# A gate matrix product by seven block products, with block sums on GpSimd, in a two-layer decoder trunk

## The chip, the cores and the metric

The kernel runs on one core of a Trainium2 chip. A core has five engines that run their own instruction queues side by side: PE (matrix products), DVE (VectorE), ACT (ScalarE), POOL (GpSimd) and SP (SyncE, which here issues the transfers). They share an on-chip memory, SBUF; PE writes to another, PSUM, in banks of 128 x 512 floats that DVE and ACT read. The metric is the time of one execution on the device in microseconds.

## The reference

The reference runs 512 tokens of width 1024 through two layers. Each layer mixes tokens (layer 0 with a state-space mixer, layer 1 with HGRN2), norms, runs a two-matrix MLP of width 4096 with a squared ReLU, norms again, and adds a gated embedding:

```
h = layer_norm(ALPHA * x + mix, ...)
h = layer_norm(ALPHA * h + sq_relu_mlp(h, w1, w2), ...)
x = h + sigmoid(h @ ple_w_gate) * (p @ ple_w_proj)
```

The change is to the last line: the gate h @ ple_w_gate is 512x1024 by 1024x1024, the embedding p @ ple_w_proj is 512x256 by 256x1024. All is float32.

## The kernel before

**A product in three matmuls.** A float32 operand is split into a high part (a cast to a reduced float32 format) and a low part (the operand less its high part). A product is three matmuls, high by high, high by low and low by high (`mm3`, L115 to L118), all accumulated in one PSUM bank. A weight arrives as 128x1024 pieces ("units"): SP loads one into a `raw` buffer, of which there are three; ACT casts it to `whi` (L110); DVE subtracts to `wlo` (L112). There are six `whi` and six `wlo` buffers.

**The MLP's second product** already goes by blocks. Two rows by two columns of blocks take seven block products in place of eight (Strassen's method in Winograd's form): sums of blocks of the weights (`weight_sums`, t1 to t4, made in place in `r` buffers) and of the activations (`half_blocks`: a11, a12, a22 and the sums s1 to s4) are multiplied, and banks accumulate several products each. All its sums are made on DVE. In the last of four rounds the layer norm of token chunks 0 and 1 (128 tokens each) starts while the last of these block products still run on PE (`after(0), after(1)`), and that of chunks 2 and 3 follows.

**The layer norm** of a chunk is a mean and a sum of squares, then two DVE operations over 128x1024 (L220, L221). Then PE transposes the chunk in eight transposes to the banks `pt` and `pm`, ACT casts each bank to the high part (L235) and DVE subtracts to the low part (L236). Chunk 0 is transposed within the last block product (`turns`), chunk 1 within the embedding products, chunks 2 and 3 within the gate's first products (`turned`).

**The gate, before.** For each half h of the 1024 columns, and each of four chunks c, 8 x 3 matmuls of 512 columns make the gate in a bank `pj`. ACT takes the sigmoid (L485), DVE multiplies with the embedding's bank (L486, where `pp` is `py` or `pj`) and adds to the accumulator `acc` (L489). The embedding product `proj` takes 2 x 3 matmuls. In layer 0 the result is turned for the next mixer (L443 to L447) one piece late; in layer 1 it goes out to memory. The very last piece in layer 1 is done in two parts of 256 columns.

**What sets the order.** Each engine runs its instructions in a fixed order, set when the kernel is built. `tc.high_priority(offset=n)` moves the instructions inside it ahead of those that were written up to n earlier: `LEAD` (100) for units, `SUMS` for weight sums, `TURN` (200) for the transposes' splits, `SOON` (40) for the norm. A buffer or bank that is reused waits until its last reader is done. POOL does nothing but fill a few constants.

Of the kernel before, what the change touches and what calls it, by code (L numbers as in the profile page):

```python
# [29 lines left out]
TURN = 200  # L30

# [10 lines left out]
def trunk(ctx: ExitStack, tc, a):  # L42
# [63 lines left out]
    def split(f, lead=LEAD):  # L106
        n = f.shape[1]
        with tc.high_priority(offset=lead):
            hi = mk(whip, [P, 1024], "whi", F32R)
            nc.scalar.copy(hi[:, :n], f)  # L110
            lo = mk(wlop, [P, 1024], "wlo", F32R)
            nc.vector.tensor_sub(lo[:, :n], f, f32(hi[:, :n]))  # L112
        return hi, lo
# [171 lines left out]

# [25 lines left out]
    def weight_sums(w, lead):  # L311
# [7 lines left out]
        with tc.high_priority(offset=lead):  # L319
            for u in range(2):  # L320
                load(0, u, w[0][1][u])
                load(2, u, w[1][1][u])
                nc.vector.tensor_sub(t[2][u], t[2][u], t[0][u])
                load(1, u, w[0][0][u])
                nc.vector.tensor_sub(t[0][u], t[0][u], t[1][u])
                nc.vector.tensor_add(t[1][u], t[2][u], t[1][u])
            for u in range(2):
                load(3, u, w[1][0][u])
                nc.vector.tensor_sub(t[3][u], t[3][u], t[1][u])
# [52 lines left out]
    def mlp_and_gate(layer, h_s, last):  # L382
# [66 lines left out]
        pps = {}  # L449

        def proj(c, pu):

            pp = pps[c] = bank(*((psj, "pj") if c > 1 and pps else (psy, "py%d" % (c % 2))))
            for k in range(2):
                ks = slice(k * 512, (k + 1) * 512)
                mm3(pp, p_s[0][:, k, c * P : (c + 1) * P], p_s[1][:, k, c * P : (c + 1) * P], pu[0][:, ks], pu[1][:, ks], k == 0, k == 1)

        for h in range(2):
            pu = unit(a[f"wp_{layer}"][h])
            gu = [unit(a[f"wg_{layer}"][4 * h + j]) for j in range(4)]  # L460
            for c in range(NCH):
                sl = slice(c * P, (c + 1) * P)
                if h == c == 0:
                    for i in range(NCH):
                        proj(i, pu)
                        if i == 1:
                            turned(1)
                if h == 1:
                    proj(c, pu)
                pp = pps.pop(c)  # L470
                pg = bank(psj, "pj")
                sg = tmp("sg", [P, T])
                parts = 2 if last and h == 1 and c == NCH - 1 else 1
                for i in range(parts):
                    n = 512 // parts
                    if i:
                        pg = bank(psj, "pj")
                    cs = slice(i * n, (i + 1) * n)
                    for k in range(8):
                        ks = slice((k % 2) * 512 + i * n, (k % 2) * 512 + (i + 1) * n)  # L480
                        mh, ml = gu[k // 2][0][:, ks], gu[k // 2][1][:, ks]
                        mm3(pg[:, cs], h_s.h(k, sl), h_s.l(k, sl), mh, ml, k == 0, k == 7)
                        if h == 0 and c < 2 and k == 2:
                            turned(c + 2)
                    nc.scalar.activation(sg[:, cs], pg[:, cs], AF.Sigmoid)  # L485
                    nc.vector.tensor_mul(sg[:, cs], pp[:, cs], sg[:, cs])  # L486
                    fs = slice(h * 512 + i * n, h * 512 + (i + 1) * n)
                    d = acc[:, c, fs]
                    nc.vector.tensor_add(d, sg[:, cs], d)  # L489
                    if last:  # L490
                        nc.sync.dma_start(a["out"][c * P : (c + 1) * P, fs], d)
                while late:
# [790 lines left out]
```

## Time and profile before

| | us |
|---|---|
| median of three runs (1422.39 to 1423.45) | 1422.39 |
| profiled execution | 1422.3 |
| its span | 1420.5 |
| PE busy | 1413.6 |
| DVE busy | 1025.4 |
| ACT busy | 744.4 |
| POOL busy | 1.6 |
| gate stage, layer 0 | 704.0 to 764.5 |
| gate stage, layer 1 | 1358 to the end |

The span runs from the first to the last instruction on the profile; the profiled execution's own time is 1.8 us longer. "Busy" is the time in which an engine had an instruction running. Several matmuls overlap, so their rate is read from the distance of their starts and not from the duration of one. A row of the profile names a line of the kernel, an engine, an operation, the output and inputs with their shapes, how many, their time and what ended the wait before them.

### The profile page before, as it was taken

Reading aid. Unit: us, or ns where it says so; the run is one execution under the profiler, and the core shown is the slowest. Engines: PE = TensorE matmul, PEld = TensorE weight load, DVE = VectorE, ACT = ScalarE, POOL = GpSimd, SP = SyncE. Lnnn points to the kernel's source line nnn. Section 1 sums busy time; section 2 is a strip of 40 time slices with the busy share of each in tenths; the row PEclk is TensorE's granted clock in tenths of the full one; section 3 lists DMA queues with packets and bytes.
Section 4 is the critical chain, followed back from the end, with each engine's and each line's share of the span. In section 5 each row is a group of like instructions: output and inputs, shape, how many; then the busy total and the mean of one; then the engine's idle time right before and its main releaser. Section 6 shows DMA issues by size and latency. Waiting matters only on the chain.

```text
span 1420.5 us, 20454 instructions
## 1 busy us (share of the span) xinstructions
PE 1413.6 (100%) x8143; PEld 1182.3 (83%) x8143; DVE 1025.4 (72%) x1713; ACT 744.4 (52%) x1089; POOL 1.6 (0%) x9
## 2 busy tenths in 40 slices
PE   9999999999999999999999999999999999999998
PEld 7888888888888888888888888888898888888887
DVE  7987777778967667677963774776785867667873
ACT  7776656664265454545543446465454544544641
POOL 0000000000000000000000000000000000000000
PEclk9999999999999999999999999999999999999999
DMA  8343333233433444442422222222163444444231
GB/s 292 127 145 108 113 118 101 95 104 124 158 119 127 156 133 149 134 148 104 149 90 91 92 92 72 90 90 76 60 238 104 148 147 135 149 133 163 89 119 45
DMA packets 48960, 174.83 MB, mean 123 GB/s; under 512 B 5728, under 2 KB 6368, under 8 KB 48736
## 3 DMA queue, kind: packets, MB, share of 16 engines
q1 hardware_dynamic: 48864, 173.52, 35.9%
q8 instruction: 64, 1.05, 0.3%
q14 instruction: 32, 0.26, 0.1%
HBM read 171.34 MB, written 2.16 MB: 122 GB/s over the span
## 4 chain that ended last, share of the span: by engine, by line
PE 96%; DVE 2%; DMA 1%; ACT 0%; issue 0%; SPq 0%
PE pj L116 25%; PE pj L118 25%; PE pj L117 25%; PE py L116 5%; PE py L118 5%; PE py L117 5%; PE py L687 1%; PE py L942 1%; PE pm L669 1%; PE py L689 1%; PE pt L635 0%; PE pt L230 0%; DMA acc<-in_xw 0%; PE pm L230 0%; DVE wlo L112 0%; DVE b L236 0%
## 5 line engine op out<-in xcount | busy, mean ns | idle before, releaser
L110 ACT CAST whi<-raw 128x1024 fp32r<-128x1024 f32 x226 | 237.1, 1050 | 377.8 <-PE pj L117 264.6
L112 DVE TENSOR_TENSOR wlo<-raw,whi 128x1024 fp32r<-128x1024 f32 x226 | 274.3, 1220 | 159.1 <-ACT whi L110 155.0
L116 PE MATMUL pj<-b,whi 128*128 128x512 f32 (+1 forms) x1008 | 381.5, 379 | 0.2 <-ACT b L235 0.2
L117 PE MATMUL pj<-b,whi 128*128 128x512 f32 (+1 forms) x1008 | 379.4, 376 | 0.7 <-DVE b L236 0.7
L118 PE MATMUL pj<-b,wlo 128*128 128x512 f32 (+1 forms) x1008 | 378.9, 376 | 0.0
L118 PE MATMUL pj<-whi,b 128*128 128x512 f32 (+1 forms) x592 | 229.5, 388 | 0.0
L116 PE MATMUL pj<-whi,b 128*128 128x512 f32 (+1 forms) x584 | 229.3, 393 | 0.0
L117 PE MATMUL pj<-wlo,b 128*128 128x512 f32 (+1 forms) x584 | 226.1, 387 | 0.0
L116 PEld LDWEIGHTS pj<-b,whi 128*128 128x128 f32 x1008 | 189.5, 188 | 36.2 <-issue 1.7
L118 PEld LDWEIGHTS pj<-b,wlo 128*128 128x128 f32 x1008 | 189.8, 188 | 34.7
L117 PEld LDWEIGHTS pj<-b,whi 128*128 128x128 f32 x1008 | 189.8, 188 | 34.6 <-DVE b L236 0.9
L118 PEld LDWEIGHTS pj<-whi,b 128*128 128x128 f32 x592 | 111.3, 188 | 22.9 <-DVE b L1137 0.2
L116 PEld LDWEIGHTS pj<-whi,b 128*128 128x128 f32 x584 | 109.8, 188 | 22.7 <-ACT k L871 0.5
L117 PEld LDWEIGHTS pj<-wlo,b 128*128 128x128 f32 x584 | 109.8, 188 | 21.2
L110 ACT CAST whi<-r 128x1024 fp32r<-128x1024 f32 x64 | 67.4, 1053 | 63.8 <-PE pj L118 35.6
L112 DVE TENSOR_TENSOR wlo<-r,whi 128x1024 fp32r<-128x1024 f32 x64 | 78.0, 1219 | 22.2 <-ACT whi L110 22.0
L118 PE MATMUL py<-whi,b 128*128 128x512 f32 x216 | 84.2, 390 | 0.0
L117 PE MATMUL py<-wlo,b 128*128 128x512 f32 x192 | 74.8, 389 | 0.0
L116 PE MATMUL py<-whi,b 128*128 128x512 f32 x192 | 74.4, 389 | 0.0
L573 DVE SCALAR_TENSOR_TENSOR cv<-pj,cst,cv 128x509 f32<-128x509 f32 (+2 forms) x66 | 49.0, 742 | 8.7 <-ACT cv L570 8.4
L118 PEld LDWEIGHTS py<-whi,b 128*128 128x128 f32 x216 | 40.5, 188 | 8.5
L116 PEld LDWEIGHTS py<-whi,b 128*128 128x128 f32 x192 | 36.1, 188 | 7.6
(321 smaller groups left out, 1816.0 us busy)
## 6 DMA issues: line engine op xcount, KB each, us to landing
raw<-in_w SPq DMA_DIRECT2D x112, 512.0 KB, 3.2
r<-in_w SPq DMA_DIRECT2D x64, 512.0 KB, 3.5
raw<-in_wssd SPq DMA_DIRECT2D x38, 512.0 KB, 3.7
a<-csd SPq DMA_DIRECT2D x16, 512.0 KB, 3.5
raw<-in_wso SPq DMA_DIRECT2D x16, 512.0 KB, 3.4
raw<-in_wg SPq DMA_DIRECT2D x16, 512.0 KB, 3.4
raw<-in_whvg SPq DMA_DIRECT2D x16, 512.0 KB, 3.3
raw<-in_whq SPq DMA_DIRECT2D x16, 512.0 KB, 3.4
```

Of the source, the lines that this page charges most:

```text
L110: nc.scalar.copy(hi[:, :n], f)
L112: nc.vector.tensor_sub(lo[:, :n], f, f32(hi[:, :n]))
L116: nc.tensor.matmul(out, sh, mh, start=start, stop=False, **kw)
L117: nc.tensor.matmul(out, sh, ml, start=False, stop=False, **kw)
L118: nc.tensor.matmul(out, sl, mh, start=False, stop=stop, **kw)
L573: nc.vector.scalar_tensor_tensor(cv[:, d:], ps[:, : T - d], convw[:, i, k : k + 1], cv[:, d:], ALU.mult, ALU.add)
L669: nc.tensor.matmul(pst_[:, c * P : (c + 1) * P], btok[:, c, :], xw[:, c].rearrange("p h q -> p (h q)"), start=True, stop=True)
L687: nc.tensor.matmul(yd[64 * r : 64 * r + 64, sl], xdt[:, c, r, :], m[:, r, sl], start=True, stop=c == 0)
L689: nc.tensor.matmul(yd[64 * r : 64 * r + 64, sl], pv[:, c - 1, r, :], ecs[:, r, (c - 1) * P : c * P], start=False, stop=True,)
L942: nc.tensor.matmul(ps[r][32 * b : 32 * b + 32, base + n * c : base + n * c + n], kk[r][:, ts], moving(r, 4 * c + b), start=True, stop=True,)
```

## The change

The gate is computed as the MLP's second product is: the token chunks 0 and 1 against 2 and 3, and the columns' halves, make 2x2 blocks, and seven block products of two chunks by 4 x 3 matmuls take the place of eight. `norm_blocks` takes the place of `norm`: it splits the transposed chunks into the blocks a11, a12, a22 and the sums s1 to s4, and keeps unsplit copies of a11 and a12 (`keep`). Weight sums t1 to t4, and their low parts, are made on POOL, as are the last subtraction for s4 and the low parts of s1 and s4. Their high parts stay casts on ACT. Two banks of the block products are copied to SBUF (`held`, `sb2`, `sb3`) to be added to others. The sequence of products is a11, a12, s3, s2, a22, s1, s4. Embedding products are put between them, and the last one, of chunk 1's second half, comes after the last gate product; its sigmoid is thus taken before it. In layer 1 that embedding product has two parts of 256 columns. The next mixer begins with chunks 2 and 3.

In the diff, lines with only "..." mark what is left out.

```diff
+GATE = 300
...
-    def split(f, lead=LEAD):
+    def split(f, lead=LEAD, eng=nc.vector):
         n = f.shape[1]
         with tc.high_priority(offset=lead):
             hi = mk(whip, [P, 1024], "whi", F32R)
             nc.scalar.copy(hi[:, :n], f)
             lo = mk(wlop, [P, 1024], "wlo", F32R)
-            nc.vector.tensor_sub(lo[:, :n], f, f32(hi[:, :n]))
+            eng.tensor_sub(lo[:, :n], f, f32(hi[:, :n]))
...
+        blk = {n: mk(b8, [P, 2, 4, 256], "b8", F32R) for n in ("a11", "a12", "a22")}
+        keep = mk(b8, [P, 2, 4, 256], "b8")
...
+        def put(name, cs, f, eng=nc.vector):
+            hi, lo = blk[name][:, 0, :, cs], blk[name][:, 1, :, cs]
+            nc.scalar.copy(hi, f)
+            eng.tensor_sub(lo, f, f32(hi))
+
+        def turned(c):
+            src = acc[:, c, :]
+            cs = slice(c % 2 * P, c % 2 * P + P)
+            pts = bank(pst, "pt"), bank(psm, "pm")
+            for q, pt in enumerate(pts):
+                for j in range(4):
+                    k = 4 * q + j
+                    nc.tensor.transpose(pt[:, j * P : (j + 1) * P], src[:, k * P : (k + 1) * P], ident)
+            v = [pt.rearrange("p (j t) -> p j t", j=4) for pt in pts]
+            with tc.high_priority(offset=TURN):
+                a11, a12 = keep[:, 0, :, cs], keep[:, 1, :, cs]
+                if c < 2:
+                    put("a11", cs, v[0])
+                    nc.scalar.copy(a11, v[0])
+                    put("a12", cs, v[1])
+                    nc.scalar.copy(a12, v[1])
+                    return
+                if not more:
+                    more.append(tmp("blk", [P, 2, 4, 256]))
+                    for n in ("s3", "s2", "s1", "s4"):
+                        blk[n] = mk(b8, [P, 2, 4, 256], "b8", F32R)
+                s1, s3 = more[0][:, 0, :, cs], more[0][:, 1, :, cs]
+                nc.scalar.copy(s1, v[1])
+                nc.vector.tensor_sub(s3, a11, v[0])
+                nc.vector.tensor_add(s1, v[0], s1)
+                put("s3", cs, s3)
+                put("a22", cs, v[1])
+                nc.vector.tensor_sub(a11, s1, a11)
+                put("s2", cs, a11)
+            nc.gpsimd.tensor_sub(a12, a12, a11)
+            put("s1", cs, s1, nc.gpsimd)
+            put("s4", cs, a12, nc.gpsimd)
...
-    def weight_sums(w, lead):
+    def weight_sums(w, lead, eng=nc.vector):
...
-                nc.vector.tensor_sub(t[2][u], t[2][u], t[0][u])
+                eng.tensor_sub(t[2][u], t[2][u], t[0][u])
...
-                    h_s, after, turned, sums = norm(2 * layer + 1)
+                    blk, after, turned, sums = norm_blocks(2 * layer + 1)
...
+        t1, t2, t3, t4 = weight_sums(w, GATE, nc.gpsimd)
+        pus, pps, held = {}, {}, {}
...
+        def product(x, f, c, ps, start, hook=None):
+            cs = slice(c * P, (c + 1) * P)
+            for k in range(4):
+                hi, lo = f[k // 2]
+                ks = slice((k % 2) * 512, (k % 2 + 1) * 512)
+                mm3(ps, blk[x][:, 0, k, cs], blk[x][:, 1, k, cs], hi[:, ks], lo[:, ks], start and k == 0, k == 3, skip_group_check=True)
+                if hook and (c, k) == (1, 1):
+                    hook()
...
+        def finish(c, h, sg):
+            while late:
+                late.pop(0)()
+            pp = pps.pop((c, h))
+            n = 512 // len(pp)
+            for i, part in enumerate(pp):
+                cs = slice(i * n, (i + 1) * n)
+                d = acc[:, c, h * 512 + i * n : h * 512 + (i + 1) * n]
+                nc.vector.tensor_mul(sg[:, cs], part, sg[:, cs])
+                nc.vector.tensor_add(d, sg[:, cs], d)
...
+        two = lambda p, tag: [bank(p, tag % c if "%" in tag else tag) for c in range(2)]
+        proj(0, 0)
+        turned(1)
+        proj(1, 0)
+        xb = two(psy, "py%d")
+        f = [unit(v) for v in w[0][0]]
+        for c in range(2):
+            product("a11", f, c, xb[c], True, lambda: turned(2))
+            held[c] = tmp("sg", [P, T])
+            nc.scalar.copy(held[c], xb[c])
+        f = [unit(v) for v in w[1][0]]
+        for c in range(2):
+            z = bank(psj, "pj")
+            product("a12", f, c, z, True, lambda: turned(3))
+            sg = held[c]
+            nc.vector.tensor_add(sg, z, sg)
+            nc.scalar.activation(sg, sg, AF.Sigmoid)
+            finish(c, 0, sg)
+        f = [split(v, LEAD, nc.gpsimd) for v in t3]
+        proj(2, 0)
+        proj(3, 0)
+        y = two(psj, "pj")
+        sb3 = mk(w4, [P, 2, T], "a")
+        for c in range(2):
+            product("s3", f, c, y[c], True)
+            nc.scalar.copy(sb3[:, c], y[c])
+        f = [split(v, LEAD, nc.gpsimd) for v in t2]
+        sb2 = mk(w4, [P, 2, T], "b")
+        for c in range(2):
+            product("s2", f, c, xb[c], False)
+            nc.scalar.copy(sb2[:, c], xb[c])
+        f = [split(v, LEAD, nc.gpsimd) for v in t4]
+        for c in range(2):
+            product("a22", f, c, y[c], False)
+            nc.vector.tensor_add(sb2[:, c], y[c], sb2[:, c])
+            nc.scalar.activation(sb2[:, c], sb2[:, c], AF.Sigmoid)
+            finish(2 + c, 0, sb2[:, c])
+        f = [split(v, LEAD, nc.gpsimd) for v in t1]
+        proj(2, 1)
+        proj(3, 1)
+        for c in range(2):
+            product("s1", f, c, xb[c], False)
+            nc.vector.tensor_add(sb3[:, c], xb[c], sb3[:, c])
+            nc.scalar.activation(sb3[:, c], sb3[:, c], AF.Sigmoid)
+            finish(2 + c, 1, sb3[:, c])
+        f = [unit(v) for v in w[1][1]]
+        for c in range(2):
+            if c == 0:
+                proj(0, 1)
+            product("s4", f, c, xb[c], False)
+            sg = tmp("sg", [P, T])
+            nc.scalar.activation(sg, xb[c], AF.Sigmoid)
+            if c:
+                proj(1, 1, 2 if last else 1)
+            finish(c, 1, sg)
...
-            for c in range(NCH):
+            for c in (2, 3, 0, 1):
```

On POOL, the order in layer 0's gate stage after the eight weight sums (`r` are the sums t1 to t4; `b_908` is `keep`, where a12 becomes the s4 sum; `b_1019` is s1 and `b_1020` is s4, split; `blk_6034` holds the unsplit s1 and s3):

```order
L113 TENSOR_TENSOR wlo_6142<-r_5932,whi_6140 128x1024
L113 TENSOR_TENSOR wlo_6146<-r_5941,whi_6144 128x1024
L113 TENSOR_TENSOR wlo_6193<-r_5935,whi_6191 128x1024
L113 TENSOR_TENSOR wlo_6197<-r_5944,whi_6195 128x1024
L333 TENSOR_TENSOR b_908_5567<-b_908_5567 128x4x128
L302 TENSOR_TENSOR b_1019_6037<-blk_6034,b_1019_6037 128x4x128
L302 TENSOR_TENSOR b_1020_6038<-b_908_5567,b_1020_6038 128x4x128
L113 TENSOR_TENSOR wlo_6228<-r_5948,whi_6226 128x1024
L333 TENSOR_TENSOR b_908_5567<-b_908_5567 128x4x128
L113 TENSOR_TENSOR wlo_6232<-r_5951,whi_6230 128x1024
L302 TENSOR_TENSOR b_1019_6037<-blk_6034,b_1019_6037 128x4x128
L302 TENSOR_TENSOR b_1020_6038<-b_908_5567,b_1020_6038 128x4x128
```

Before, POOL had no instruction between its constants and the next mixer's first fill. The second low part of t4 and the second s4 subtraction stand among the low parts of s1 and s4.

On ACT, in the same stage around the first sigmoids, before (L485 is the sigmoid of a chunk, L235 the cast of a transposed bank, L446 that of the late turn):

```order
L216 ACTIVATE lnsd_5911<-lnmv_5910,cst_165 128x1
L485 ACT_TABLE_LOAD
L485 ACTIVATE sg_6001<-pj_6000 128x512
L235 CAST b_904_5563<-pt_6011 128x4x128
L235 CAST b_905_5564<-pm_6012 128x4x128
L235 CAST b_904_5563<-pt_6054 128x4x128
L235 CAST b_905_5564<-pm_6055 128x4x128
L485 ACTIVATE sg_6044<-pj_6043 128x512
L446 CAST b_986_5924<-pt_6086 128x4x128
```

and now (L301 is the cast in `put`, `b_1018` is s2, `b_1017` s3 and `b_907` a22; L326 a copy of a transposed bank; L558 the sigmoid, here that of chunk 1):

```order
L301 CAST b_1018_6036<-b_908_5567 128x4x128
L326 COPY blk_6034<-pm_6099 128x4x128
L301 CAST b_1017_6035<-blk_6034 128x4x128
L301 CAST b_907_5566<-pm_6099 128x4x128
L301 CAST b_1019_6037<-blk_6034 128x4x128
L301 CAST b_1020_6038<-b_908_5567 128x4x128
L111 CAST whi_6226<-r_5948 128x1024
L111 CAST whi_6230<-r_5951 128x1024
L301 CAST b_1018_6036<-b_908_5567 128x4x128
L301 CAST b_1019_6037<-blk_6034 128x4x128
L301 CAST b_1020_6038<-b_908_5567 128x4x128
L558 ACTIVATE sg_6060<-sg_6060 128x512
```

The sigmoid of chunk 1 stood right behind the casts of the transposed banks; it now stands behind the two casts of s4 (`b_1020`), whose input is `b_908` from POOL, and two casts of t4.

On DVE, at the norm of chunks 0 and 1, before (L112 is the low part of a weight unit, L358 the addition of a block product to the accumulator with its sum):

```order
L220 SCALAR_TENSOR_TENSOR acc_99<-acc_99,lnmv_5790,a_5559 128x1024
L112 TENSOR_TENSOR wlo_5944<-raw_5940,whi_5942 128x1024
L112 TENSOR_TENSOR wlo_5950<-raw_5946,whi_5948 128x1024
L218 RECIPROCAL lnrs_5786<-lnsd_5777 128x1
L218 RECIPROCAL lnrs_5800<-lnsd_5791 128x1
L358 ISA acc_99,lnsum_5567<-pj_5817,acc_99 128x512
L358 ISA lnsum_5567 128x1
L221 SCALAR_TENSOR_TENSOR acc_99<-acc_99,lnrs_5786,b_5560 128x1024
L221 SCALAR_TENSOR_TENSOR acc_99<-acc_99,lnrs_5800,b_5560 128x1024
L112 TENSOR_TENSOR wlo_5956<-raw_5952,whi_5954 128x1024
```

and now (each line number is one higher up to here; L409 is what L358 was):

```order
L219 RECIPROCAL lnrs_5786<-lnsd_5777 128x1
L221 SCALAR_TENSOR_TENSOR acc_99<-acc_99,lnmv_5790,a_5559 128x1024
L219 RECIPROCAL lnrs_5800<-lnsd_5791 128x1
L222 SCALAR_TENSOR_TENSOR acc_99<-acc_99,lnrs_5786,b_5560 128x1024
L222 SCALAR_TENSOR_TENSOR acc_99<-acc_99,lnrs_5800,b_5560 128x1024
L113 TENSOR_TENSOR wlo_5996<-raw_5992,whi_5994 128x1024
L113 TENSOR_TENSOR wlo_6002<-raw_5998,whi_6000 128x1024
L302 TENSOR_TENSOR b_905_5564<-pt_5868,b_905_5564 128x4x128
L409 ISA acc_99,lnsum_5563<-pj_5817,acc_99 128x512
L409 ISA lnsum_5563 128x1
```

The two low parts of gate weights that stood ahead of the norm's last operations stand behind them.

More of the change, by code (lines that the diff above doesn't have):

```diff
@@ L447, in turn @@
             nc.vector.tensor_sub(x_n.lo[h][:, :, sl], v, f32(hh))
[L449 to L460, printed above, removed]
-            for c in range(NCH):
[L462 to L492, printed above, removed]
-                    late.pop(0)()
-                if not last:
-                    late.append(lambda h=h, c=c: turn(h, c))
@@ new lines, in mlp_and_gate, with proj @@
+        wg = a[f"wg_{layer}"]
+        w = [[[wg[4 * j + 2 * i + u] for u in range(2)] for j in range(2)] for i in range(2)]
+        t1, t2, t3, t4 = weight_sums(w, GATE, nc.gpsimd)
+        pus, pps, held = {}, {}, {}
+        def proj(c, h, parts=1):
+            if h not in pus:
+                pus[h] = unit(a[f"wp_{layer}"][h])
+            pu = pus[h]
+            pps[c, h] = []
+            n = 512 // parts
+            for i in range(parts):
+                pp = bank(psj, "pj")[:, :n]
+                for k in range(2):
+                    ks = slice(k * 512 + i * n, k * 512 + (i + 1) * n)
+                    mm3(pp, p_s[0][:, k, c * P : (c + 1) * P], p_s[1][:, k, c * P : (c + 1) * P], pu[0][:, ks], pu[1][:, ks], k == 0, k == 1)
+                pps[c, h].append(pp)
@@ new lines, in product @@
+        def product(x, f, c, ps, start, hook=None):
[16 more added lines that the diff above has]
+                nc.vector.tensor_add(d, sg[:, cs], d)
+                if last:
+                    nc.sync.dma_start(a["out"][c * P : (c + 1) * P, h * 512 + i * n : h * 512 + (i + 1) * n], d)
+            if not last:
+                late.append(lambda: turn(h, c))
```

15 lines of the change are left out of this document (11 added, 4 removed).

## Prediction

> **What bounds the kernel now.** I read the totals and the chain of waits first, then the totals of the stretches around the first layer's gate, then single rows there.
>
> ```profile
> span 1420.5 us, 20454 instructions
> PE 1413.6 (100%) x8143; PEld 1182.3 (83%) x8143; DVE 1025.4 (72%) x1713; ACT 744.4 (52%) x1089; POOL 1.6 (0%) x9
> PE 96%; DVE 2%; DMA 1%; ACT 0%; issue 0%; SPq 0%
> ```
>
> TensorE (PE) is busy the whole span and carries 96% of the chain: a matmul taken away is time won, unless PE then waits. GpSimd (POOL) has done 1.6 us of work in 1420.5. The profiled execution took 1422.3 us, 1.8 around its span; the median of the runs, 1422.39, is the same within 0.1, so I sum against 1422.3.
>
> ```profile
> core 0: us, PE busy (x) PEld busy (x) DVE busy (x) ACT busy (x) POOL busy (x), PEclk, DMA share, GB/s
> 664.00:675.00 11.00, 11.00 (x50) 8.88 (x49) 10.87 (x16) 7.93 (x10) 0.53 (x1) 1.00 0.14 48
> 675.00:686.00 11.00, 11.00 (x50) 9.13 (x49) 10.20 (x13) 4.43 (x5) 0.00 (x0) 1.00 0.31 101
> 686.00:698.00 12.00, 12.00 (x54) 9.94 (x54) 9.29 (x18) 7.53 (x13) 0.00 (x0) 1.00 0.56 190
> 698.00:704.00 6.00, 6.00 (x31) 5.01 (x31) 6.00 (x9) 3.16 (x6) 0.50 (x1) 1.00 0.56 190
> 704.00:764.50 60.50, 60.50 (x294) 50.25 (x293) 36.19 (x53) 24.87 (x42) 0.03 (x1) 1.00 0.22 74
> ```
>
> The gate stage of layer 0 is 704.0 to 764.5. In it DVE is 60% busy, but in the 40 us before it 36.4 (10.87 + 10.20 + 9.29 + 6.00): the work that the change prepares there meets an engine with 3.6 us to spare. The clock was 1.00 throughout.
>
> **The matmuls removed.** Before, a layer's gate is 2 halves x 4 chunks x 8 x 3 = 192 matmuls; seven block products of 2 chunks x 4 x 3 are 168. Their pace stands in two rows 24 matmuls apart:
>
> ```profile
> 692.39 0.39 PE L116 MATMUL pj<-whi,b 128*128 128x512 f32 x1
> 697.84 0.39 PE L116 MATMUL py<-whi,blk 128*128 128x512 f32 x1
> 703.28 0.60 PE L230 MATMUL pt<-cst,acc 128*128 128x128 f32 x4
> 704.07 0.48 PE L116 MATMUL pj<-whi,a 128*128 128x512 f32 x1
> ```
>
> (697.84 − 692.39)/24 = 0.227 us, not the 0.39 of one row, since they overlap. 24 fewer are 5.45 us per layer, 10.9 in both. A chunk's eight transposes take 704.07 − 703.28 = 0.8, four about 0.45; their number is unchanged. The reads of PSUM and the casts that the block sums need run on ACT and DVE beside PE, except where a stall is named below.
>
> **The tail.** Before, the last half chunk is done in two halves of 256 columns, and the end is sigmoid, multiply, add, transfer:
>
> ```profile
> 1413.58 0.28 PE L118 MATMUL pj<-whi,b 128*128 128x256 f32 x1
> 1416.10 0.28 PE L118 MATMUL pj<-whi,b 128*128 128x256 f32 x1
> 1416.42 0.38 ACT L485 ACTIVATE sg<-pj 128x256 f32<-128x256 f32 x1 [2.49 <-PE pj L118]
> 1416.83 0.42 DVE L486 TENSOR_TENSOR sg<-py,sg 128x256 f32<-128x256 f32 x1 [1.99 <-ACT sg L485]
> ```
>
> Narrow matmuls cost (1416.10 − 1413.58)/21 = 0.12. The 48 narrow gate matmuls (5.76) become 24 wide (5.45), a gain of 0.31; six wide of the last embedding product become twelve narrow, a loss of 0.08. With that product last, its sigmoid is done under it: 0.41 (1416.83 − 1416.42) leaves the tail, of which I leave 0.15 for hand-overs that come nearer together. Layer 1 wins 0.23 + 0.25 = 0.48.
>
> **GpSimd's new work.** Per layer POOL now makes eight weight sums and eight low parts of 128x1024 and six operations of 128x512. The trace has no two-input operation on POOL; the nearest rows are its memsets:
>
> ```profile
> L804 POOL MEMSET sc<- 128x512 f32 x2 | 1.1, 528 | 701.9 <-PE pj L118 672.5 <-PE py L118 29.4
> L184 POOL MEMSET cm<- 128x128 f32 x1 | 0.2, 204 | 0.0
> ```
>
> The slope is (528 − 204)/384 = 0.84 ns an element, with 0.10 fixed. A memset makes one pass, writing; a subtraction reads two operands and writes one. Lower bound, one pass: 0.96 for 1024 and 0.53 for 512. Upper bound, three passes: 2.69 and 1.40. Below one pass nothing is likely, since it writes as much. Two passes are 1.83 and 0.97. I take the middle of two and three, X = 2.3 and Y = 1.2, since two reads that don't overlap fully with a write lie there. The Trainium skill, "GPSIMD Engine Reference", section 3.1, gives 4497 ns for an fp32 add of 2048 elements on GpSimd, so an estimate of 2.25 for 1024; by it the total below would fall by 0.1, and no run here shows it.
>
> **Stall 1, the first transposes.** Around the layer norm of chunks 0 and 1, DVE has now:
>
> ```profile
> 693.21 2.36 DVE L112 TENSOR_TENSOR wlo<-raw,whi 128x1024 fp32r<-128x1024 f32 x2
> 695.68 1.28 DVE L220 SCALAR_TENSOR_TENSOR acc<-acc,lnmv,a 128x1024 f32<-128x1024 f32 x1
> 696.87 0.68 DVE L358 CUSTOM_DVE_ANT_0 acc<-pj,acc 128x512 f32<-128x512 f32 x1
> 697.55 1.28 DVE L220 SCALAR_TENSOR_TENSOR acc<-acc,lnmv,a 128x1024 f32<-128x1024 f32 x1
> 698.75 2.35 DVE L112 TENSOR_TENSOR wlo<-raw,whi 128x1024 fp32r<-128x1024 f32 x2
> 701.75 2.48 DVE L221 SCALAR_TENSOR_TENSOR acc<-acc,lnrs,b 128x1024 f32<-128x1024 f32 x2
> ```
>
> One split of each pair goes behind the norm's last rows or away. Then the norm of chunk 0 starts at 694.5 and ends (1.2 + 0.6 + 1.2 + 1.2, with gaps) near 699.1. PE now transposes chunk 0 after the first twelve matmuls of the last block product, at 697.84 + 12 x 0.227 = 700.56: 1.4 of slack. The moved split ends at 694.5 + 1.2 + 0.6 + 1.2 + 2.4 + 1.14 + gaps = 701.5, and only then does its raw buffer, one of three, come free for the next gate weight.
>
> ```profile
> raw<-in_wg SPq DMA_DIRECT2D x16, 512.0 KB, 3.4
> r<-in_w SPq DMA_DIRECT2D x64, 512.0 KB, 3.5
> 702.12 1.06 ACT L110 CAST whi<-raw 128x1024 fp32r<-128x1024 f32 x1 [2.54 <-PE py L118]
> 704.91 0.59 ACT L235 CAST b<-pm 128x512 fp32r<-128x512 f32 x1
> ```
>
> Landing at 701.5 + 3.4 = 704.9, the cast ends near 706.0. On ACT the copy of chunk 0's second transposed bank stands behind that cast and ends near 706.5. PE wants the bank for chunk 1's transposes at about 706.1: 0.4 to 0.5 lost, so 0.5 (bounds 0, if the transfer lands earlier, and 1.6, if it lands 1 us later). SP issues six more transfers of 512 KB per layer. They land in the stretch where the transfer engines were 0.56 busy, so I give them nothing; queued together they would add that same 1 us.
>
> **Stall 2, the sigmoid behind GpSimd.** On ACT the sigmoid of chunk 1's first half is now queued behind the cast of s4's second half, whose input is a subtraction on POOL; POOL does that behind low parts of s1, s4 and t4. DVE's multiply waits for the sigmoid, and it frees the bank in which PE's s3 product of the second chunk starts.
>
> ```profile
> 716.24 1.28 ACT L485 ACT_TABLE_LOAD   x1 [2.79 <-PE pj L118]
> 717.53 0.60 ACT L485 ACTIVATE sg<-pj 128x512 f32<-128x512 f32 x1
> 718.03 0.58 ACT L235 CAST b<-pt 128x512 fp32r<-128x512 f32 x1
> 1409.94 0.69 DVE L486 TENSOR_TENSOR sg<-py,sg 128x512 f32<-128x512 f32 x1 [5.38 <-ACT sg L485]
> ```
>
> Count from T, the first matmul of the a12 product. PE: its 24 matmuls, sixteen transposes and twelve matmuls of the next embedding products end at T + 9.8 (36 x 0.227 + 2 x 0.8); twelve each of s3 and s2 for the first chunk and a turn of four transposes later (5.9) it wants the bank, at T + 15.7. ACT: the weight slot of a12's first unit comes free six matmuls into its second chunk, at T + 2.7 + 0.8 + 1.4 = 4.9; the cast into it (1.0), the table load (1.28), the sigmoid (0.6) and five casts or copies at 0.5, the last of them s1's first, end at T + 10.4 with hand-overs. POOL then makes the low parts of s1 and s4 for the first chunk, one low part of t4 and the second s4 subtraction, 3Y + X; cast, sigmoid, multiply and hand-overs add 0.58 + 0.60 + 0.69 + 0.1 = 2.0. PE waits 10.4 + 3Y + X + 2.0 − 15.7 = 3Y + X − 3.3 = 2.6 us. Bounds: nothing at one pass (2.55 − 3.3), 3.6 at three; 1.4 at two. Queued on ACT behind that sigmoid are a turn's cast and the casts of t1, all more than 5 us ahead of PE's need; I find no third wait up to the stage's end. Layer 1 has no turn there, but two matmuls more, and the same queue.
>
> Layer 0's last turn is hidden: the next mixer begins with chunks 2 and 3, whose 24 matmuls (5.45) cover sigmoid, multiply, add, transposes and split, about 3.7.
>
> **Sum.** 10.9 + 0.48 won, 2 x (0.5 + 2.6) = 6.2 lost: 5.2 won, 1422.3 − 5.2 = **1417.1**, say 1417.0. Its own range is 1414 (POOL at two passes) to 1419.5 (three, and half a microsecond later transfers).
>
> **Rival B: DVE and GpSimd hold each other up (slower).** The sum lets POOL run beside DVE free of charge. The trace has two overlaps, each with a memset:
>
> ```profile
> 673.55 0.53 POOL L804 MEMSET sc<- 128x512 f32 x1 [672.48 <-PE pj L118]
> 703.50 0.53 POOL L804 MEMSET sc<- 128x512 f32 x1 [29.42 <-PE py L118]
> 664.97 1.23 DVE L112 TENSOR_TENSOR wlo<-r,whi 128x1024 fp32r<-128x1024 f32 x1
> 673.27 2.57 DVE L112 TENSOR_TENSOR wlo<-r,whi 128x1024 fp32r<-128x1024 f32 x2
> L362 DVE TENSOR_TENSOR acc<-py,acc 128x512 f32<-128x512 f32 x5 | 3.3, 678 | 0.0
> ```
>
> The two splits under the first took 2.57 against 2 x 1.23, the two L221 under the second (at 701.75, above) 2.48 against the L220's 2 x 1.28: little or nothing, but a memset reads nothing. If both engines' reads of two SBUF operands took turns, POOL's 8 x 2.3 = 18.4 us before the stage would have to fit into DVE's 3.6 idle and the some 13 operations that read PSUM (like the five of 3.3 us, about 9 us): 5.8 are left over (18.4 − 3.6 − 9), and after the 1.4 of slack PE starts the gate 4.4 late. In the stage, one low part lies within the norm of chunks 2 and 3 (1.8 of its 2.3, the rest under PSUM reads), and stall 2 grows by the four DVE operations of 0.6 that its POOL queue meets, 2.4. That is 8.6 per layer on top of A's net: 1417.1 + 17.2 = **1434**. From a shared loss of 2.6 per layer the gain is gone; from 4.0 the kernel is measurably slower. For it: DVE's rows there stand back to back, and nearly all read two SBUF operands. Against it: no row shows it. The Trainium skill, "SBUF — State Buffer", section "Who interferes with whom", states that a DVE instruction with two SBUF inputs contends with a GpSimd instruction that reads SBUF, and not with one that only writes. The memset agrees with the second half; the first no run shows. It speaks against this change.
>
> **Rival C: GpSimd as fast as its memset.** One pass: stall 2 is gone, 11.4 − 1.0 = 10.4 won, **1412**. For it stands the memset's slope, against it the two operands that a memset doesn't read.
>
> **Rival D: no measurable change.** Three passes (3.6) and the late transfer with stall 1 at 1.1: 2 x 4.7 = 9.4 lost of 11.4, **1420.3**; a mild contention of 2 to 3 us per layer ends there too.
>
> **How the numbers follow.** A gets 0.50, since its terms are counts at measured paces and no row shows two engines in each other's way. B gets 0.38: the place where POOL's sums fall is the one where DVE has 3.6 us left in 40, so a third of the priced contention would eat the gain, and the memsets, which read nothing, don't clear it. C gets 0.05, D 0.07. About 0.2% (2.8 us) is what a measurement of this kernel can tell from no change. Faster (under 1419.5): most of A, 0.47, and C, 0.52. Slower (over 1425.2): B, 0.38. The rest, D and A's edge, is 0.10. The range runs from just under C's 1412 to just above B's 1434: 1411 to 1436, with A's own 1414 to 1419.5 inside.
>
> **What would show it.** Matmuls: 24 of 512 columns fewer per layer in the gate, at the same 0.227. POOL: rows of 128x1024 between 1.8 and 2.7 (over 3 would lengthen stall 2 one for one). Stall 2: PE idle at the first matmul of the second s3 chunk, put down to DVE's multiply, about 2.6; if nothing is idle there, C. Stall 1: PE idle at chunk 1's transposes after ACT's copy. B: DVE's splits of 1.22 rising towards 2 to 3.5 wherever a POOL row overlaps, and PE idle before the chunk-0 transposes. The forecast is wrong if PE waits in the 40 us before the stage, or if a sum on POOL is late for its first cast.

## The result and the profile after

The changed kernel takes 1462.99 us (median of five runs, 1461.01 to 1463.61) against 1422.39 us before: slower by a ratio of 1.0281, with a 95% interval of 1.0266 to 1.0296. That is 40.6 us, where the forecast was a gain of 5 and the slower rival said 12 lost. The totals and the chain of waits of the changed kernel:

```profile
span 1461.8 us, 20483 instructions
PE 1416.6 (97%) x8077; PEld 1177.6 (81%) x8077; DVE 1092.4 (75%) x1737; ACT 774.4 (53%) x1136; POOL 111.6 (8%) x53
PE 82%; DVE 12%; ACT 3%; issue 2%; DMA 1%; POOL 1%; ACTq 0%; DVEq 0%
```

PE had 6.9 us without work before (1420.5 − 1413.6) and has 45.2 now (1461.8 − 1416.6): 38.3 of the 41.3 that the span grew. It is also busy 3.0 us longer, though some 11.1 us of matmuls are gone, so those that are left took about 14 us longer. DVE, at 2% of the chain before, now holds 12%.

Where in layer 0? The first row is the transposes of chunk 0; the other two are the first and last start of one matmul of the next mixer, of the kernel before and of the changed one:

```profile
714.04 0.66 PE L311 MATMUL pt<-cst,acc 128*128 128x128 f32 x4 [1.83 <-DVE acc L222]
...
L942 PE MATMUL py<-qx,k x256: 232/233/258, 799.5 to 956.7; 128*32 128x80 f32 x128
...
L1043 PE MATMUL py<-qx,k x256: 232/233/257, 820.6 to 977.9; 128*32 128x80 f32 x128
```

The prediction had these transposes at 700.56, and in the run below without the sums they start at 700.80: 13.5 us (714.04 − 700.56) are lost before the gate stage begins. The mixer starts 21.1 us late although 5.45 us of matmuls fell away, so the stage lost another 13. Layer 1 accounts for the other 20 us (41.3 − 21.1).

Now DVE and POOL side by side in the 40 us before the gate, from the timeline of the changed kernel (start, duration, engine):

```profile
665.50 3.19 POOL L374 TENSOR_TENSOR r<-r,r 128x1024 f32<-128x1024 f32 x1 [664.43 <-DMA r<-in_wg]
669.82 3.35 POOL L376 TENSOR_TENSOR r<-r,r 128x1024 f32<-128x1024 f32 x1 [1.13 <-DMA r<-in_wg]
673.25 2.67 POOL L377 TENSOR_TENSOR r<-r,r 128x1024 f32<-128x1024 f32 x1
...
692.70 3.25 POOL L377 TENSOR_TENSOR r<-r,r 128x1024 f32<-128x1024 f32 x1
```

and of DVE:

```profile
665.21 1.23 DVE L113 TENSOR_TENSOR wlo<-r,whi 128x1024 fp32r<-128x1024 f32 x1
666.35 2.89 DVE L354 TENSOR_TENSOR a<-a 128x512 f32<-128x512 f32 x1
...
670.90 2.82 DVE L355 TENSOR_TENSOR a<-b,a 128x512 f32<-128x512 f32 x1
673.65 2.83 DVE L348 TENSOR_TENSOR blk<-a,blk 128x512 fp32r<-128x512 f32 x1
...
693.63 0.68 DVE L413 TENSOR_TENSOR acc<-pj,acc 128x512 f32<-128x512 f32 x1
```

An operation of 0.68 us with two operands from SBUF takes 2.8 to 2.9: L354, due at 666.35, ends at 669.24, and POOL's operation beside it ran from 665.50 to 668.69: the 0.55 that are left are near L354's own 0.68, as if it began only when POOL was done. The last row is the counterpart: L413 has one operand from PSUM (`pj`), lies wholly inside POOL's row of 692.70 to 695.95, and takes its 0.68 as ever. The row of L348 is what PE waits for:

```profile
670.51 0.40 PE L117 MATMUL pj<-whi,blk 128*128 128x512 f32 x1
676.53 0.80 PE L119 MATMUL pj<-whi,blk 128*128 128x512 f32 x1 [5.62 <-DVE blk L348]
677.13 0.63 PE L117 MATMUL pj<-whi,blk 128*128 128x512 f32 x1
...
681.39 0.63 PE L119 MATMUL pj<-whi,blk 128*128 128x512 f32 x1
```

In the kernel before, where L348 is L297, the same split ended at 669.74 and PE's matmul started at 669.80, so there was no room for a delay:

```profile
669.06 0.68 DVE L297 TENSOR_TENSOR blk<-a,blk 128x512 fp32r<-128x512 f32 x1
669.80 0.49 PE L118 MATMUL pj<-whi,blk 128*128 128x512 f32 x1
```

In the changed kernel PE stands still for 5.62 us, and from 677.13 to 681.39 ten matmuls follow 0.426 apart, not 0.227. The totals by stretch show the granted clock (third column from the end; the columns are those of the prediction's table):

```profile
670.00:675.00 5.00, 0.91 (x3) 0.43 (x3) 5.00 (x3) 0.62 (x1) 4.92 (x2) 1.00 0.60 210
675.00:680.00 5.00, 3.47 (x8) 2.79 (x9) 5.00 (x7) 1.65 (x2) 0.93 (x1) 0.55 0.00 0
680.00:685.00 5.00, 5.00 (x18) 3.94 (x18) 2.25 (x3) 2.50 (x3) 0.00 (x0) 0.76 0.17 50
```

PE's waits of both layers, by line and releaser (total, times, longest):

```profile
PE pj L119 <- DVE blk L348: 11.2, 2, 5.6
PE pt L311 <- DVE acc L222: 6.7, 4, 1.8
PE pt L494 <- DVE acc L536: 4.1, 2, 3.3
PE pj L117 <- DVE sg L535: 3.4, 1, 3.4
...
PE pm L311 <- ACT b L319: 2.8, 2, 1.4
```

Nearly all are waits for DVE, spread from the MLP's last block split to the gate's middle. None stands in this view for the kernel before.

### The profile page after: what moved, and what is told of

The parts are those of the page before. It is cut to its first block, busy times and chain, and to the rows that moved or that the text cites. A ratio compares the mean times of both kernels' runs of the same rounds, so it can differ in the third digit from the quotient of the medians.

```text
span 1461.8 us, 20483 instructions
## 1 busy us (share of the span) xinstructions
PE 1416.6 (97%) x8077; PEld 1177.6 (81%) x8077; DVE 1092.4 (75%) x1737; ACT 774.4 (53%) x1136; POOL 111.6 (8%) x53
## 4 chain that ended last, share of the span: by engine, by line
PE 82%; DVE 12%; ACT 3%; issue 2%; DMA 1%; POOL 1%; ACTq 0%; DVEq 0%
PE pj L117 22%; PE pj L119 21%; PE pj L118 21%; PE py L119 4%; PE py L118 4%; PE py L117 4%; DVE wlo L113 3%; DVE acc L222 1%; PE py L788 1%; PE py L1043 1%; DVE acc L221 1%; DMA raw<-in_wssd 1%; ACT whi L111 1%; PE pm L770 1%; DVE b L302 1%
## 5 line engine op out<-in xcount | busy, mean ns | idle before, releaser
L113 DVE TENSOR_TENSOR wlo<-raw,whi 128x1024 fp32r<-128x1024 f32 x222 | 280.7, 1271 | 166.3 <-ACT whi L111 156.8
L119 PE MATMUL pj<-whi,b 128*128 128x512 f32 x530 | 207.1, 391 | 0.0
L117 PE MATMUL pj<-whi,b 128*128 128x512 f32 x496 | 197.6, 399 | 4.4 <-DVE sg L535 3.4
L118 PE MATMUL pj<-wlo,b 128*128 128x512 f32 x496 | 194.1, 392 | 0.0
L111 ACT CAST whi<-r 128x1024 fp32r<-128x1024 f32 x80 | 84.0, 1053 | 74.0 <-PE pj L119 46.1
L119 PEld LDWEIGHTS pj<-whi,b 128*128 128x128 f32 x530 | 100.0, 189 | 21.1 <-DVE b L1238 0.2
L117 PEld LDWEIGHTS pj<-whi,b 128*128 128x128 f32 x496 | 93.4, 188 | 25.8 <-DVE sg L535 3.8
L118 PEld LDWEIGHTS pj<-wlo,b 128*128 128x128 f32 x496 | 93.6, 189 | 18.4
L374 POOL TENSOR_TENSOR r<-r,r 128x1024 f32<-128x1024 f32 x4 | 11.7, 2936 | 1263.6 <-DMA r<-in_wg 1263.6
L117 PE MATMUL py<-whi,b 128*128 128x512 f32 x256 | 100.2, 393 | 1.9 <-DVE acc L413 1.9
L118 PE MATMUL py<-wlo,b 128*128 128x512 f32 x256 | 100.5, 393 | 0.0
L119 PE MATMUL py<-whi,b 128*128 128x512 f32 x256 | 100.2, 391 | 0.0
L117 PEld LDWEIGHTS py<-whi,b 128*128 128x128 f32 x256 | 48.4, 189 | 12.9 <-DVE acc L413 2.7
L119 PEld LDWEIGHTS py<-whi,b 128*128 128x128 f32 x256 | 48.5, 189 | 10.2
```

Of the source, the lines that this page charges most:

```text
L113: eng.tensor_sub(lo[:, :n], f, f32(hi[:, :n]))
L117: nc.tensor.matmul(out, sh, mh, start=start, stop=False, **kw)
L118: nc.tensor.matmul(out, sh, ml, start=False, stop=False, **kw)
L119: nc.tensor.matmul(out, sl, mh, start=False, stop=stop, **kw)
L374: eng.tensor_sub(t[2][u], t[2][u], t[0][u])
```

## The experiments

Two theories were to be told apart. **C** (collision): POOL's operations read SBUF, and while one runs DVE cannot get its second SBUF operand. **Q** (queues): the new order of products, banks and engine queues costs the time, and POOL is merely slow. Theory C is the mechanism of the prediction's rival B (and not its rival C, the fast memset). Each engine's order is set anew when a kernel is built, so an edit can also move instructions that it doesn't touch; where that bears on a reading, the text says so.

### GpSimd's reads alone, beside the kernel before

The kernel before got operations on POOL that nothing waits for, in the stretch where the changed kernel makes its sums. The other two runs have `memset(xa, 0.0)` and `tensor_copy(xa, xa)` in the place of the subtraction:

```diff
+    def extra(n, src):
+        nc.gpsimd.tensor_copy(xt[-1][:, 0:1], src)
+        xa = xt[-1]
+        for _ in range(n):
+            nc.gpsimd.tensor_sub(xa, xa, xa)
...
+            extra(x, f32(blk["a12"][:, 0, 2 * p, 0:1]))
...
+                extra(10, d[:, 0:1])
...
+                                half_blocks(blocks[g], *zs, p, 6 if g == 3 and p == 1 else 0)
```

> The kernel before, with 16 idle-purpose subtractions of 128x512 on GpSimd per layer (a scratch tile less itself; nothing reads it), 6 from the time that the last MLP block is split and 10 after its third block product. Theory C: some 22 us of GpSimd rows in a stretch where VectorE has 3.6 us free; VectorE rows beside them grow from 0.68 and 1.22 by up to 1.4, and the kernel takes 1434 to 1450 us. Theory Q: no engine waits for them, so 1422.4 within 1.5.

> The same as the run with the subtractions, with a memset of the same tile in place of each: the same instructions in the same places, but none reads SBUF. Theory C (reads collide): 1422.4 within 1.5, VectorE rows unchanged. Theory Q: the same. If any GpSimd work slows VectorE or PE, it is over 1426 here too.

> The kernel before with 16 copies of 128x512 on GpSimd per layer in the places of the subtractions (scratch tile onto itself): one operand read in place of two. If any GpSimd read of SBUF keeps VectorE from its second operand: VectorE rows beside them grow by up to the length of a copy, and the time is 1426 to 1442. If only two-operand GpSimd operations do: 1422.4 within 1.5.

Measured: 1445.14 us with subtractions (ratio 1.016, 1.0144 to 1.0175), 1422.60 with memsets (1.0001, 0.9991 to 1.001), 1430.43 with copies (1.0053, 1.0037 to 1.007). Rows of POOL and DVE with the subtractions:

```profile
664.95 9.67 POOL L295 TENSOR_TENSOR xa<-xa 128x512 f32<-128x512 f32 x6
...
666.79 2.06 DVE L112 TENSOR_TENSOR wlo<-r,whi 128x1024 fp32r<-128x1024 f32 x1
668.77 1.52 DVE L313 TENSOR_TENSOR a<-a 128x512 f32<-128x512 f32 x1
```

with the memsets:

```profile
663.49 3.46 POOL L295 MEMSET xa<- 128x512 f32 x6
...
664.54 1.23 DVE L112 TENSOR_TENSOR wlo<-r,whi 128x1024 fp32r<-128x1024 f32 x1
665.68 0.69 DVE L313 TENSOR_TENSOR a<-a 128x512 f32<-128x512 f32 x1
```

and with the copies:

```profile
664.19 7.12 POOL L295 COPY xa<-xa 128x512 f32<-128x512 f32 x6
...
665.63 1.63 DVE L112 TENSOR_TENSOR wlo<-r,whi 128x1024 fp32r<-128x1024 f32 x1
667.18 1.10 DVE L313 TENSOR_TENSOR a<-a 128x512 f32<-128x512 f32 x1
```

The same two DVE operations take 1.23 and 0.69 beside memsets, 1.63 and 1.10 beside copies, 2.06 and 1.52 beside subtractions. POOL's being busy costs nothing; its reading SBUF does, with one operand too, and the more the longer it reads. All three times lie where C put them. DVE's order through this stretch is the same in all three kernels (against the kernel before a few splits moved by some places, which costs the run with memsets nothing), so C is shown, without one line of the change. Q can't explain a loss between kernels of one order.

### The change with GpSimd as slow, but not reading

```diff
+FILLS = 3
...
+    class Filled:
+        def tensor_sub(self, o, x, y):
+            e = (lambda v: v[:, 0:1, 0:1]) if len(o.shape) == 3 else (lambda v: v[:, 0:1])
+            nc.gpsimd.tensor_sub(e(o), e(x), e(y))
+            for _ in range(FILLS):
+                nc.gpsimd.memset(o if o.dtype == F32 else f32(o), 0.0)
...
-        t1, t2, t3, t4 = weight_sums(w, GATE, nc.gpsimd)
+        t1, t2, t3, t4 = weight_sums(w, GATE, filled)
```

and so for the low parts and the block sums; `e` takes the first column of a tile.

> The changed kernel with each of GpSimd's 22 operations per layer replaced by the same operation on one column (so that it waits for what it waited for) and three memsets of its whole output, so that GpSimd is as long at work (3 x 0.96 us for 1024 columns) and its results come as late, but hardly reads SBUF; the sums are zeros and the gate is not the reference's. Forecast A as put on record: 1422.4 - 11.4 + 2 x (0.5 + stall 2), where X = 3.2 and Y = 1.8 make stall 2 up to 5.3 us; 1412 to 1423, VectorE rows at 1.22 and 0.68. Theory C needs this to fall under 1425 too. Theory Q (the lateness of GpSimd's results, not the collision): 1450 or more.

Measured: 1418.44 us, ratio 0.9973 (0.9963 to 0.9982). Groups of POOL and DVE (DVE from 660 to 765 us), and PE's two waits after 640 us:

```profile
L106 POOL MEMSET wlo<- 128x1024 f32 x48 | 45.4, 955 | 0.9
...
L125 DVE TENSOR_TENSOR wlo<-raw,whi 128x1024 fp32r<-128x1024 f32 x18 | 21.8, 1222 | 10.7 <-POOL b L104 5.1 <-PE pj L131 3.4 <-ACT whi L123 2.2
...
PE pj L129 <- DVE b L588: 2.7, 2, 2.0
PE pt L506 <- DVE acc L548: 1.6, 1, 1.6
```

With POOL at least as long at work (121.9 us busy, against 111.6 in the changed kernel) but hardly reading, the same order of products is 4.0 us faster than the kernel before. DVE's splits take 1.222. The zeros don't speed PE up: its matmuls start 0.227 us apart here too. Ahead of layer 0's gate DVE's order is that of the changed kernel, and chunk 0's transposes start at 700.93, not 714.04. Within the gate ACT's order differs too: above all, the sigmoid of chunk 1 stands ahead of the last cast of s4, so the stall of 3.4 us in layer 1 that hangs on this order in the changed kernel (its wait for L535) can't arise. What is left of the difference, 1462.99 − 1418.44 = 44.6 us, is the price of the collisions (and of the clock that they cost PE). Q falls.

### The order alone, with the sums left out

Everything on DVE, without the weight sums (`None`: the loads alone) and their low parts (`high`: the cast alone, for t1 to t4):

```diff
-        t1, t2, t3, t4 = weight_sums(w, GATE, nc.gpsimd)
+        t1, t2, t3, t4 = weight_sums(w, GATE, None)
...
-        f = [split(v, LEAD, nc.gpsimd) for v in t3]
+        f = [high(v) for v in t3]
```

> All on VectorE, and the eight weight sums and the eight low parts of the summed weights per layer are left out (the weights are used as loaded, their high part in place of the low part), so the gate is not the reference's; every load, cast, product, bank and queue of the change stays. If VectorE's and GpSimd's work for the sums is the whole loss and the prediction's count of matmuls and tail holds: 1422.4 - 10.9 - 0.5 and up to 2 for stall 1, so 1410 to 1415 us. If the order of products, banks and queues waits by itself (theory Q): over 1425.

Measured: 1413.67 us, ratio 0.9937 (0.9922 to 0.9952), 9.0 us won of the 11.4 that matmuls and tail were priced at. PE's only waits after 640 us are 1.1 in all:

```profile
PE py L123 <- ACT b L307: 1.1, 2, 0.5
```

So the products, banks and queues of the change lose little: 2.4 us of the 11.4, of which 1.1 are these waits and the rest is not explained. What is lost beyond that is lost by making the sums.

### The sums on VectorE, whole and in part

With all 22 operations per layer on DVE (`nc.gpsimd` replaced by `nc.vector`); with the weight sums alone on DVE; with the weight sums alone on POOL; and with all on DVE and `GATE = 0`:

> The changed kernel with all 22 operations per layer back on VectorE, nothing else edited. Theory C (GpSimd's two-operand operations keep VectorE from its second SBUF operand): 22 operations of 1.2 or 0.6 us on VectorE, 23 us per layer, replace 56 us of GpSimd rows that VectorE waited behind; VectorE is still overfull before the gate by 5.5 us, so 1424 to 1436 us, VectorE rows back at 1.22 and 0.68, and PE's longest wait before the gate under 3 us. Theory Q (the new order of products, banks and queues costs the time, and GpSimd is merely slow): the waits stay where they are, 1450 us or more.

> Only the eight weight sums per layer go back to VectorE; low parts and block sums stay on GpSimd. Theory C: the 24 us of GpSimd work ahead of the gate is gone, so of the 13.5 us that chunk 0's transposes came late some 8 return, the 13 us lost within the gate stage stay: 1443 to 1450 us. Theory Q: the loss ahead of the gate stays, as VectorE was full there: within 5 us of 1463.

> Only the eight weight sums per layer on GpSimd, low parts and block sums on VectorE. Theory C: chunk 0's transposes are as late as with the whole change (about 13 us per layer), and within the gate stage the loss is as with all on VectorE (about 10): 1450 to 1462. If the sums on GpSimd alone were harmless and the low parts were the trouble: under 1442.

> All on VectorE as in the run that took 1439.2, with the weight sums no longer moved ahead of other work (GATE = 0): they stand around and behind the layer norm of chunks 0 to 3 in place of ahead of it. If VectorE's lack of room ahead of the gate is what is left of the loss: 4 to 5 us per layer come back, 1429 to 1433. If VectorE lacks room within the gate stage too, what is won ahead is lost behind: 1436 to 1446.

| per layer, on POOL | us | ratio, interval |
|---|---|---|
| all 22 (the change) | 1462.99 | 1.0281, 1.0266 to 1.0296 |
| the 8 weight sums | 1455.49 | 1.0229, 1.0214 to 1.0244 |
| the 8 low parts and 6 block operations | 1447.80 | 1.0182, 1.0167 to 1.0197 |
| none | 1439.21 | 1.0116, 1.0099 to 1.0132 |
| none, sums behind the norm | 1436.75 | 1.0100, 1.0084 to 1.0115 |

With one part on POOL the times lie where C put them (1450 to 1462 with the sums there, 1443 to 1450 with the rest). Both parts cost, the sums 16.3 us (1455.49 − 1439.21), the rest 8.6 (1447.80 − 1439.21), together 24.9, where the change is 23.8 slower than all on DVE. A few us of such differences may come of orders that changed along: with all on DVE, for one, ACT copies a bank (L572) ahead of the first sigmoid, in the changed kernel behind it. Work that takes DVE 23 us is cheaper there than POOL's 55 us of reading ((111.6 − 1.6)/2). But without any collision the weight sums and their low parts still cost 25.5 us in both layers (1439.21 − 1413.67), more than the 9.0 that the products win. The run with all on DVE missed its expectation of 1424 to 1436: I had counted only the room ahead of the gate. PE's longest waits there, and with the sums behind the norm:

```profile
PE pj L119 <- DVE blk L348: 5.2, 2, 2.6
PE pt L311 <- DVE blk L328: 4.3, 2, 2.2
...
PE py L117 <- ACT b L301: 9.7, 4, 3.6
PE py L118 <- DVE wlo L113: 8.0, 2, 4.3
```

Moved behind the norm, the sums no longer hold up the MLP's split (no wait for L348), but the low parts come late within the gate (8.0), and so do ACT's casts (9.7), the longest of them (3.6) behind a sum that DVE makes. That is the second case of its expectation: DVE lacks the room on both sides. In that run it is busy for 39.76 of the 40 us ahead of the gate and 30.58 of the 31 that follow (the third busy time; the columns are those of the prediction's table):

```profile
664.00:704.00 40.00, 40.00 (x181) 32.99 (x180) 39.76 (x60) 23.27 (x33) 0.00 (x0) 1.00 0.60 194
704.00:735.00 31.00, 21.62 (x94) 16.14 (x94) 30.58 (x45) 20.70 (x37) 0.00 (x0) 0.82 0.14 46
```

None of these versions beats the kernel before.

### Shorter operations on GpSimd

```diff
+    class Halves:
+        def __init__(self, f):
+            self.f = f
+
+        def __call__(self, o, x, y):
+            n = 2 if len(o.shape) == 3 else o.shape[1] // 2
+            for s in (slice(0, n), slice(n, 2 * n)):
+                self.f(o[:, s], x[:, s], y[:, s])
```

> The changed kernel with each GpSimd operation cut into two of half the columns; the same elements, the same places. If the loss is GpSimd's total time in the shared path: 1463 within 4. If it is what one operation holds VectorE up for (VectorE gets in between two operations): a wait is half as long, and of the 40 us lost 10 to 20 come back, 1442 to 1453.

Measured: 1449.52 us, ratio 1.0185 (1.017 to 1.0201): 13.5 us come back. DVE gets its turn between two operations of POOL, so halving them about halves what one DVE operation waits (L354's counterpart took 1.78, not 2.89). In this kernel too the sigmoid of chunk 1 stands ahead of the last cast of s4, so up to 3.4 of the 13.5 us may be due to that order. POOL itself took longer over the sums, since it waits for DVE as well:

```profile
L107 POOL TENSOR_TENSOR r<-r,r 128x512 f32<-128x512 f32 x32 | 58.9, 1876 | 1261.3 <-DMA r<-in_wg 1261.3
...
PE pj L132 <- DVE blk L361: 9.4, 2, 5.3
```

The 58.9 us stand against 49.9 for the same sums uncut (11.7 + 13.0 + 11.8 + 13.4, four groups of the changed kernel). The longest wait ahead of the gate stays: what PE needs there lies behind several operations of DVE, each taking turns.

### The last embedding product alone

The kernel before, with the gate's last half chunk whole and the last embedding product behind it in two parts:

> The kernel before with only the last part of the change: the last chunk's second gate half as one product of 512 columns, its sigmoid, and the last embedding product behind it in two parts of 256. The prediction's terms for it: 0.23 by the matmuls and 0.25 by the sigmoid, 1421.9; within what can be told from no change.

Measured: 1421.98 us in eleven runs against 1422.46, ratio 0.9997 (0.9989 to 1.0006). By the time it can't be told from no change, as expected. Its last matmul starts at 1415.75 and the span is 1419.9, so the tail behind it is some 4.15 us, where it was 4.40 (1420.5 − 1416.10; the spans are read to a tenth):

```profile
1415.75 0.28 PE L118 MATMUL pj<-whi,b 128*128 128x256 f32 x1
```

## Why the prediction was wrong

**The choice of the likeliest case.** This step failed first. Forecast A let POOL run beside DVE "free of charge" and got 0.50 because "no row shows two engines in each other's way". The trace had no row in which POOL read SBUF, so it could not have shown it; the silence of a view that has no instance says nothing. The Trainium skill, "SBUF — State Buffer", section "Who interferes with whom", did say that a DVE instruction with two SBUF inputs contends with a GpSimd instruction that reads SBUF, and not with one that only writes. The runs agree with both halves: rows with two SBUF operands grow beside subtractions (0.69 to 1.52), and memsets cost nothing (1422.60). Rows with an operand from PSUM keep their 0.68.

**A, as a kernel without collisions, came near, in part by luck.** The run in which POOL fills in place of reading took 1418.44 against the 1417.0 on record. But of the 11.4 us that A counted as won, 9.0 were won with the sums left out, and of its 6.2 us of stalls that run shows none where A put them and 4.3 elsewhere (L588 and L548); the two misses roughly make up for each other. The pace of 0.227 holds, and the tail's 0.25 is measured as some 0.25. A's own range was slightly mis-summed: its terms for two passes, and for three with the later transfers (1422.3 − 11.4 + 2 x 1.9 and + 2 x 4.6), give 1414.7 and 1420.1, not 1414 and 1419.5.

**GpSimd's price.** X = 2.3 and Y = 1.2 were slightly small. The shortest rows, where DVE is not in the way, are 2.39 and 1.27; with collisions the means are 2.67 for low parts and up to 3.37 for sums:

```profile
738.26 2.39 POOL L113 TENSOR_TENSOR wlo<-r,whi 128x1024 fp32r<-128x1024 f32 x1 [3.84 <-ACT whi L111]
...
L380 POOL TENSOR_TENSOR r<-r,r 128x1024 f32<-128x1024 f32 x4 | 13.4, 3372 | 0.0
```

**Stall 1** was forecast at 0.5 and is the wait of the banks `pm` for ACT's copy L319, 1.4 per layer in the changed kernel. It came of the collisions too: with POOL's fills in place of its reads, PE's waits don't have it.

**Stall 2** was forecast at 2.6 with its whole chain, and layer 1 shows that chain link by link, at 3.4:

```profile
1427.16 0.62 ACT L301 CAST b<-b 128x512 fp32r<-128x512 f32 x1 [2.79 <-POOL b L333]
1427.68 0.62 ACT L558 ACTIVATE sg<-sg 128x512 f32<-128x512 f32 x1
...
1429.09 0.50 PE L117 MATMUL pj<-whi,b 128*128 128x512 f32 x1 [3.37 <-DVE sg L535]
```

In layer 0 PE had by then waited longer for something else (3.3 for L536, ahead of a turn), and the stall was covered.

**Rival B's mechanism was right and its size wrong**: 8.6 us per layer on top of A, where the runs give 22.3 (44.6/2). The term that failed is "5.8 are left over, and after the 1.4 of slack PE starts the gate 4.4 late"; chunk 0's transposes came 13.5 late. Three things were wrong in it.
- It let POOL's reading fill DVE's idle time over all 40 us. POOL's operations came when their loads landed, three from 665.5 to 675.9 and five from 686.6 to 702.6. Beside the first three DVE got six operations done from 665.21 to 676.4, in 11.2 us; two splits at 1.14 and four at 0.6 take 4.7 alone.
- It let PE notice only at the norm. PE was waiting already for the MLP's own split, L348, which is just in time in the kernel before and came 5.6 late.
- It took PE's clock as given. Matmuls behind the long waits ran 0.2 us slower each. The granted clock is 0.50 there for some 19 us of PE's work (676.5 to 682.4, 750.6 to 754.1, 1352.0 to 1358.2 and 1429.9 to 1433.3); at 0.427 a matmul that is an estimated 44 matmuls, and 9 of the 14 us by which those that are left took longer over both layers. Where the rest lies was not followed up.

It also sized the POOL work ahead of the gate at 18.4; the eight rows sum to 25.1 us (3.19 + 3.35 + 2.67 + 2.64 + 3.27 + 3.25 + 6.71).

**Rivals C and D** are out: neither one pass nor a mild contention is what the rows show. What stays open is how the two engines' turns are decided; rows show alternation mostly, and POOL operations stretched by DVE's as DVE's by POOL's, and no run here looked closer.

## What to carry to other kernels

GpSimd is not a free third vector engine. Beside an operation of it that read SBUF, a DVE operation with two SBUF operands waited here, for up to 2.2 us (0.68 became 2.89). So where DVE is near full, work moved from DVE to GpSimd can cost DVE more than it saves: here 23 us of DVE work per layer became 55 us of GpSimd reading. Before such a move, count DVE's two-SBUF-operand rows in the stretch where the moved work will land, and find the nearest PE need behind them; in these runs only GpSimd operations that write (memsets), or DVE operations with an operand from PSUM, went undisturbed. And when saving matmuls by adding sums, price the sums against the idle time of the engine that makes them: 5.45 us of PE per layer was bought with 23 us on an engine that had not so much to spare, and that lost with or without GpSimd.

## What the runs showed of the hardware

**Reads with one operand collide too.** GpSimd copies, at 0.93 us for 512 columns, stretched DVE's 0.69 to 1.10 and cost the kernel 7.7 us (1430.43 − 1422.69, the kernel before beside it). A memset of 0.53 cost nothing.

**PE's clock falls after pauses of little over 2 us**, and I had put no price on it. Matmul starts are 0.227 us apart at a granted clock of 1.00 and 0.42 to 0.43 at 0.50. In the profiles with waits, PE came out of single pauses of 1.0 to 2.05 us at 0.23, and out of most from 2.2 us upward at 0.43, for up to 14 matmuls, some 6 us. The length alone doesn't decide: pauses of 2.2 and 2.6 also ended at 0.23 (with all on DVE, one of 2.6 in layer 1 did so, and its like in layer 0 not), and with the weight sums alone on POOL two of 1.2 close together were followed by 0.43. A clear case, with no other long pause near, stands in the run with copies, where the pace is 0.427 over six intervals from 673.47 to 676.03:

```profile
672.52 0.50 PE L118 MATMUL pj<-whi,blk 128*128 128x512 f32 x1 [2.28 <-DVE blk L305]
...
673.47 0.63 PE L118 MATMUL pj<-whi,blk 128*128 128x512 f32 x1
...
676.03 0.63 PE L116 MATMUL pj<-whi,blk 128*128 128x512 f32 x1
```

The stalls of 5.6 us thus cost PE some 8 each: the wait, and about 0.2 us on each of the 12 or 13 matmuls that follow.
